# S5 read-out with the chunks as the stationary operand, in two 64-column halves, and transposes behind the GELU

## The chip, the cores and the metric

The kernel runs on one core of one Trainium2 chip. Its time is the device time of one execution, in microseconds (us); the comparison later is between medians of several runs. The engines are named as in the profile: PE is TensorE's matmul side and PEld its weight loads, DVE is VectorE, ACT is ScalarE, POOL is GpSimd, SP is SyncE. POOL and SP issue DMA transfers here. TensorE's clock is granted at one of two levels, 2.4 GHz (1.0 in the profile) or 1.2 GHz (0.5).

## The reference, cut to what matters

Two layers, sequence 512, model width 2048, everything in float32. Each layer normalises and modulates `x`, projects it, runs two branches side by side (S5 state space and differential attention), and projects back. The change lies in the S5 branch:

```python
_, states = lax.associative_scan(combine, (a_seq, bu), axis=1)
c_mat = lax.complex(c_re, c_im)
y = jnp.einsum('gpn,bsgn->bsgp', c_mat, states).real + d_skip * uf
y = jax.nn.gelu(y.reshape(bsz, s, SSM_WIDTH))
ab = y @ w_glu + b_glu
out = ab[..., :SSM_WIDTH] * jax.nn.sigmoid(ab[..., SSM_WIDTH:])
```

There are 64 groups of 16 channels. The kernel cuts the 512 positions into 64 chunks of 8. For one group it needs a 128 x 64 result: 128 rows are 8 positions by 16 channels, 64 columns are the chunks. That result is the sum of two products with a contraction over 128: a table `Mb` (128 x 128, what the inputs of the same chunk give) times the inputs `U` (128 x 64), and a table `O` (128 x 128) times the states `X` at the chunks' starts (128 x 64).

## The kernel before, in words

The order of the work is written by hand. A step (`step`) belongs to one weight unit, a 512 KB tile of weights: SP loads it, ACT rounds it (`hi`), DVE takes the remainder (`lo`), and PE does 24 matmuls with 512 moving columns against it. Units are split three ahead of their use (`NH = 4` buffers). Beside that stream run generators, the S5 branch, the attention and the adaLN modulation. Each advances by one `yield` in each of three phases of a step: ahead of the split, ahead of the matmuls, and behind them. Generators are served by priority, and every engine executes its instructions in the order in which they were recorded.

The read-out is the last part of `s5_state_gen`. It takes the 64 groups in 8 rounds of 8, one round per step; each layer has 8 rounds, so there are 16 in all. In round j:

- In the first phase POOL issues three loads for the next round (`s5_load_be`, `load_m`, `s5_load_u`), and DVE makes the two tables in four operations of 1024 columns: two products and their difference for `O`, and the masking of `Mb`.
- In the second phase `gelu(j - 1)` reads the round before from its PSUM bank (rounds alternate between bank 3 and bank 2): ACT squares and scales, DVE multiplies, ACT takes the tanh, DVE forms the result in `g2`, POOL writes it to DRAM (`yD`).
- In the third phase, behind the 24 matmuls of the step, PE does 16 matmuls of the round: for each of 8 groups `Mb` stationary with `U` moving, then `O` stationary with `X` moving, 64 moving columns each. A float32 matmul shows as two records in the trace, each with its own weight load.

Behind round 7 the generator does one more GELU and sets `o.done`. `ada_chain` waits for `o.done`, then starts `ada_gen` for the gate: a 1 MB broadcast load (`in_bgate`) on POOL, 512 KB loads (`in_wada`) on SP, and DVE sums (`ada_acc`: two operations of 512 columns per tile). The attention of the same layer is running by then. For each head it projects k, q and a gate; `qk_out` copies k or q from PSUM and has SP move its rows by four DMAs (`sb<-sb`), `rope` rotates it on DVE, `qk_split` writes the pieces (`qk`) that the score matmuls read.

Elsewhere in the kernel, at the start of layer 0, `first_cols` uses matmuls with 32 stationary columns that write to the four quarters of a bank's partitions (shown as 128*32 in the trace).

Of the kernel before, what the change touches and what calls it, by code (L numbers as in the profile page):

```python
# [14 lines left out]
AF = mybir.ActivationFunctionType  # L15
# [6 lines left out]
P = 128  # L22
KT = D // P
NG = 64
# [32 lines left out]
SHARED = 8192  # L57
# [10 lines left out]
class Prog:  # L68
# [42 lines left out]
    def v(self, off, n):  # L111
        return self.sb[:, off:off + n]
# [226 lines left out]
def build(ctx, tc, io):  # L339
    q = Prog(ctx, tc, io)  # L340
    nc = q.nc
    M, A, SUB = ALU.mult, ALU.add, ALU.subtract
    v = q.v
    bank = q.bank
# [32 lines left out]
    def layout(base, limit, **sizes):  # L377
        r = Names()
        o = base
        for name, (count, n) in sizes.items():  # L380
            got = []
            for _ in range(count):
                got.append(o)
                o += n
            setattr(r, name, got if count > 1 else got[0])
        assert o <= base + limit, (o - base, limit)
        return r
# [9 lines left out]
    s5 = layout(R5, 4416, U=(2, 512), BE=(2, 384), K=(2, 128), D=(2, 128), PR=(1, 512),  # L397
                PI=(1, 512), GR=(1, 512), GI=(1, 512), A8=(1, 64))
# [3 lines left out]
    s5.A, s5.T = ra.p[0], ra.wt[0] - 128  # L402
    s5.tab = [RA + 2048 + 64 * i for i in range(24)]
    s5.tw = RA + 3584
    sh = layout(0, SHARED, X=(1, NG * 65), A=(1, 1024), B=(2, 1024))

    gl = layout(R5, 4416, gate=(1, D), g=(2, 512), zs=(2, 512))
    yst_o = [RA + 2048 + 512 * i for i in range(8)]
# [219 lines left out]
    def s5_load_be(l, j, lo):  # L628
        q.dma(v(s5.BE[j % 2], 384), io["be"][l, j, :, lo:lo + 384])

    def s5_load_u(l, j):
        src = q.uD[l][j * P:(j + 1) * P, :].rearrange("(g q) (s c) -> (q s) g c", q=16, c=64)
        q.dma(v(s5.U[j % 2], 512).rearrange("p (g c) -> p g c", c=64), src)
# [137 lines left out]
    def s5_state_gen(l):  # L771

        o = S5[l]
        todo = got = 0
        while o.v < 8:
            yield
            if todo > o.v:
                j = o.v
# [11 lines left out]
            j = o.v  # L790
            if j < 8 and o.u > j and o.r > j:
                U = v(s5.U[j % 2], 512)
# [7 lines left out]
        X = o.X  # L800
# [19 lines left out]
        for i, job in enumerate(jobs):  # L820
# [13 lines left out]
            lv, g0, gn, src, dst, n = job  # L834
# [22 lines left out]
        def load_m(j):  # L857
            base = q.kD[l][16384 * j:16384 * (j + 1)]
            src = bass.AP(base.tensor, base.offset, [[16, P], [2048, 8], [1, P]])
            q.dma(o.B[j % 2].rearrange("p (g f) -> p g f", g=8), src)  # L860
# [6 lines left out]
        def gelu(j):  # L867

            b = bank[3 - j % 2]
            g1, g2 = v(s5.g1, 512), v(s5.g2, 512)  # L870
            q.act(g1, b, AF.Square)
            q.act(g1, g1, AF.Copy, scale=0.044715, bias=1.0)
            q.tt(g1, g1, b, M)
            q.act(g1, g1, AF.Tanh, scale=math.sqrt(2.0 / math.pi))
            q.stt(g2, g1, 1.0, b, A, M)
            dst = q.yD[l][8 * j:8 * j + 8].rearrange("g r c -> r g c")
            q.dma(dst, g2.rearrange("p (g c) -> p g c", c=64))

        for j in range(8):
            if j < 7:  # L880
                s5_load_be(l, j + 1, 128)
                load_m(j + 1)
                s5_load_u(l, j + 1)
            be = v(s5.BE[j % 2], 384).rearrange("p (f g q) -> p f g q", f=3, g=8)
            O = o.A[j % 2]
            On4 = O.rearrange("p (g s e) -> p g s e", g=8, s=8)
            T4 = o.T.rearrange("p (g s e) -> p g s e", g=8, s=8)
            pr = PR[:, 8 * j:8 * j + 8, :].unsqueeze(3).to_broadcast([P, 8, 8, 16])
            pi = PI[:, 8 * j:8 * j + 8, :].unsqueeze(3).to_broadcast([P, 8, 8, 16])
            q.tt(On4, pr, be[:, 1].unsqueeze(2).to_broadcast([P, 8, 8, 16]), M)  # L890
            q.tt(T4, pi, be[:, 2].unsqueeze(2).to_broadcast([P, 8, 8, 16]), M)
            q.tt(O, O, o.T, SUB)
            Mb = o.B[j % 2].rearrange("p (g f) -> p g f", g=8)
            q.tt(Mb, Mb, tapb.unsqueeze(1).to_broadcast([P, 8, P]), M)
            yield
            if j > 0:
                gelu(j - 1)
            yield
            b = bank[3 - j % 2]
            U = v(s5.U[j % 2], 512)  # L900
            for g in range(8):
                q.mm(b[:, g * 64:(g + 1) * 64], Mb[:, g], U[:, g * 64:(g + 1) * 64], True, False)
                q.mm(b[:, g * 64:(g + 1) * 64], O[:, g * P:(g + 1) * P], X[:, 8 * j + g, 0:64], False, True)
            yield
        o.read = True
        yield
        gelu(7)
        o.done = True
        yield
        yield  # L910
# [263 lines left out]
    def layer(l):  # L1174
        u0 = l * UL
        last = l == DEPTH - 1
        o = S5[l]
# [45 lines left out]
        def start_s5():  # L1223
            t = q.shared(SHARED, F32, f"ss{l}")
            o.X = t[:, sh.X:sh.X + NG * 65].rearrange("p (g c) -> p g c", c=65)
            o.A = [t[:, sh.A:sh.A + 1024], v(s5.A, 1024)]
            o.T = v(s5.T, 1024)
            o.B = [t[:, b:b + 1024] for b in sh.B]
            o.gen = s5_gen(l)
            o.sgen = s5_state_gen(l)  # L1230
            q.spawn(1, o.gen, True)
            q.spawn(2, o.sgen, True)
# [47 lines left out]
        for j in range(first_u, 8):  # L1280
            b = next_bank()
# [7 lines left out]
        for j in range(8):  # L1289
            b = bank[(1, 0, 7)[j % 3]]  # L1290
# [53 lines left out]
        for h in range(8):  # L1344
# [6 lines left out]
            for kind in range(3):  # L1351
                b = next_bank()
# [351 lines left out]
```

## Time and profile before

| | |
|---|---|
| median of 3 runs | 1929.06 us (1927.9 to 1932.54) |
| profiled execution | 1930.6 us, of it 1928.8 us span |
| PE busy | 1898.0 us, 98% |
| DVE busy | 1352.2 us, 70% |
| ACT busy | 782.8 us, 41% |
| POOL busy | 200.5 us, 10% |
| mean granted TensorE clock | 0.994 |
| read-out rounds, layer 0 | 368.6 to 436.1 us |
| read-out rounds, layer 1 | 1274.0 to 1340.9 us |

Busy time counts an engine as busy as long as any of its instructions is in flight. Matmuls overlap, so the mean duration of one (0.39 us for 512 columns) is longer than the distance from one start to the next (0.23 us). The distance between starts, not the duration, tells what a matmul costs on PE.

### The profile page before, as it was taken

Reading aid. Unit: us, or ns where it says so; the run is one execution under the profiler, and the core shown is the slowest. Engines: PE = TensorE matmul, PEld = TensorE weight load, DVE = VectorE, ACT = ScalarE, POOL = GpSimd, SP = SyncE. Lnnn points to the kernel's source line nnn. Section 1 sums busy time; section 2 is a strip of 40 time slices with the busy share of each in tenths; the row PEclk is TensorE's granted clock in tenths of the full one; section 3 lists DMA queues with packets and bytes.
Section 4 is the critical chain, followed back from the end, with each engine's and each line's share of the span. In section 5 each row is a group of like instructions: output and inputs, shape, how many; then the busy total and the mean of one; then the engine's idle time right before and its main releaser. Section 6 shows DMA issues by size and latency. Waiting matters only on the chain.

```text
span 1928.8 us, 27771 instructions
## 1 busy us (share of the span) xinstructions
PE 1898.0 (98%) x10376; PEld 1613.2 (84%) x10376; DVE 1352.2 (70%) x2590; ACT 782.8 (41%) x1473; POOL 200.5 (10%) x316
## 2 busy tenths in 40 slices
PE   7999999999999999999999999999999999999998
PEld 4678998888888888888998899888788878888887
DVE  7748767987777887688776435796688777653444
ACT  4333234444445554322264224433344445432222
POOL 0003220231000000100001210032000000000000
PEclk8999999999999999999999999999999999999999
DMA  9967553677666964777444433376666584355233
GB/s 353 403 250 250 183 148 95 212 198 219 184 186 187 224 191 166 277 278 231 141 156 148 135 110 108 100 234 203 179 187 199 175 202 133 120 166 200 98 90 119
DMA packets 120695, 358.75 MB, mean 186 GB/s; under 512 B 32272, under 2 KB 32848, under 8 KB 118128
## 3 DMA queue, kind: packets, MB, share of 16 engines
q1 hardware_dynamic: 97776, 277.14, 45.0%
q0 software_dynamic: 22784, 79.84, 13.9%
q8 instruction: 81, 1.33, 0.3%
q14 instruction: 54, 0.44, 0.1%
HBM read 309.60 MB, written 30.54 MB: 176 GB/s over the span
## 4 chain that ended last, share of the span: by engine, by line
PE 87%; DVE 6%; DMA 3%; issue 2%; ACT 1%; SPq 0%; POOL 0%; ACTq 0%; DVEq 0%; POOLq 0%
PE bk L145 86%; DVE lo L130 2%; DVE sb L139 2%; PE bk L153 1%; DVE sb L130 1%; DMA sb<-yD 1%; DMA sb<-sb 1%; DMA sb<-in_ssm_d 0%; DMA sb<-in_wada 0%; DVE sb L134 0%; ACT sd L127 0%; DMA sb<-in_lstep 0%; ACT hi L127 0%; ACT hth L127 0%; DVE x L134 0%
## 5 line engine op out<-in xcount | busy, mean ns | idle before, releaser
L130 DVE TENSOR_TENSOR lo<-sb,hi 128x1024 fp32r<-128x1024 f32 x288 | 351.2, 1222 | 365.8 <-ACT hi L127 349.5
L127 ACT ACTIVATE hi<-sb 128x1024 fp32r<-128x1024 f32 x288 | 304.0, 1059 | 558.8 <-PE bk L145 442.2
L145 PE MATMUL bk<-hth,hi 128*128 128x512 f32 x1280 | 512.7, 401 | 0.0
L145 PE MATMUL bk<-hth,lo 128*128 128x512 f32 x1280 | 500.3, 391 | 0.0
L145 PE MATMUL bk<-htl,hi 128*128 128x512 f32 x1280 | 499.5, 390 | 0.0
L145 PE MATMUL bk<-hi,hth 128*128 128x256 f32 (+1 forms) x1088 | 360.1, 331 | 4.5 <-ACT hth L127 4.1
L145 PE MATMUL bk<-lo,hth 128*128 128x256 f32 (+1 forms) x1088 | 356.0, 327 | 0.5 <-DVE lo L130 0.5
L145 PE MATMUL bk<-hi,htl 128*128 128x256 f32 (+1 forms) x1088 | 356.1, 327 | 0.0
L139 DVE SCALAR_TENSOR_TENSOR sb<-sb 128x512 f32<-128x512 f32 (+8 forms) x633 | 296.1, 473 | 21.4 <-DMA sb<-in_wada 1.8
L145 PEld LDWEIGHTS bk<-hth,lo 128*128 128x128 f32 x1280 | 240.8, 188 | 51.9
L145 PEld LDWEIGHTS bk<-htl,hi 128*128 128x128 f32 x1280 | 241.3, 189 | 49.1 <-issue 1.9
L145 PEld LDWEIGHTS bk<-hth,hi 128*128 128x128 f32 x1280 | 241.3, 189 | 48.2 <-issue 1.9
L130 DVE TENSOR_TENSOR sb<-sb 128x4 f32<-128x4 f32 (+8 forms) x455 | 219.6, 500 | 28.3 <-DMA sb<-sb 10.9
L145 PEld LDWEIGHTS bk<-hi,hth 128*128 128x128 f32 x1088 | 207.1, 190 | 34.4 <-issue 12.0
L145 PEld LDWEIGHTS bk<-hi,htl 128*128 128x128 f32 x1088 | 207.0, 190 | 18.1 <-DVE htl L130 0.5
L145 PEld LDWEIGHTS bk<-lo,hth 128*128 128x128 f32 x1088 | 207.2, 190 | 17.4 <-DVE lo L130 0.7
L145 PE MATMUL bk<-gt,hi 128*128 128x512 f32 x512 | 159.6, 393 | 0.0
L145 PE MATMUL bk<-sb 128*128 128x128 f32 (+5 forms) x932 | 134.0, 338 | 4.3 <-DVE sb L433 3.6
L127 ACT ACTIVATE sb<-bk,sb 128x512 f32<-128x512 f32 (+3 forms) x144 | 77.2, 541 | 132.7 <-DVE sb L134 131.0
L145 PEld LDWEIGHTS bk<-gt,hi 128*128 128x128 f32 x512 | 94.7, 188 | 18.8
L127 ACT ACTIVATE sb<-bk 128x512 f32<-128x512 f32 (+3 forms) x213 | 87.8, 445 | 45.1 <-PE bk L145 35.4
L145 PE MATMUL bk<-gt,lo 128*128 128x512 f32 x256 | 99.8, 390 | 0.0
(116 smaller groups left out, 1744.0 us busy)
## 6 DMA issues: line engine op xcount, KB each, us to landing
sb<-in_w SPq DMA_DIRECT2D x288, 512.0 KB, 4.0
sb<-in_wada SPq DMA_DIRECT2D x185, 512.0 KB, 5.0
sb<-uD POOLq DMA_DIRECT2D x32, 256.0 KB, 6.0
ss<-kD POOLq DMA_DIRECT2D x16, 512.0 KB, 5.9
sb<-sb SPq DMA_DIRECT2D x128, 64.0 KB, 3.9
qk<-qk POOLq DMA_DIRECT2D x32, 256.0 KB, 4.0
sb<-in_be POOLq DMA_DIRECT2D x32, 192.0 KB, 4.3
x<-in_x SPq DMA_DIRECT2D x4, 1024.0 KB, 10.0
```

What stands on the lines that cost most here:

```text
L127: self.nc.scalar.activation(out=out, in_=in_, func=func, **kw)
L130: self.nc.vector.tensor_tensor(out=out, in0=a, in1=b, op=op)
L139: self.nc.vector.scalar_tensor_tensor(out=out, in0=a, scalar=s, in1=b, op0=op0, op1=op1)
L145: return self.nc.tensor.matmul(out, lhsT=l, rhs=r, start=a, stop=z)
L153: return self.nc.tensor.transpose(out, in_, self.ident)
```

## The change

The two operands of each read-out matmul change places: `U` and `X` (128 x 64) become stationary, `Mb` and `O` (128 columns) move. A group's result is now 64 x 128, chunks on the partitions. Of two neighbouring groups the even one is written to partitions 0 to 63 and the odd one to 64 to 127 of the bank, so the two use different 64-column halves of the array. The number of matmuls stays 16 per round.

The GELU is elementwise and works on the bank as it is. Its result then has the wrong layout for `yD`, so four 128 x 128 transposes on PE (`gelu_turn`) write it to the same bank, ACT copies it to a new tile `Y` (`gelu_out`), and POOL sends it from there. `gelu_turn` of a round stands one step later than its GELU, behind the matmuls of the next round. Behind round 7 this takes one more step, and `o.done` is set one step later.

```diff
-    sh = layout(0, SHARED, X=(1, NG * 65), A=(1, 1024), B=(2, 1024))
+    sh = layout(0, SHARED, X=(1, NG * 65), A=(1, 1024), B=(2, 1024), Y=(1, 512))
...
             q.stt(g2, g1, 1.0, b, A, M)
+
+        def gelu_turn(j):
+            for p in range(4):
+                q.tr(bank[3 - j % 2][:, P * p:P * p + P], v(s5.g2 + P * p, P))
+
+        def gelu_out(j):
+            q.act(o.Y, bank[3 - j % 2], AF.Copy)
             dst = q.yD[l][8 * j:8 * j + 8].rearrange("g r c -> r g c")
-            q.dma(dst, g2.rearrange("p (g c) -> p g c", c=64))
+            q.dma(dst, o.Y.rearrange("p (g c) -> p g c", c=64))
...
-            yield
+            if j > 1:
+                gelu_turn(j - 2)
+            yield
+            if j > 1:
+                gelu_out(j - 2)
             if j > 0:
                 gelu(j - 1)
             yield
...
-            for g in range(8):
-                q.mm(b[:, g * 64:(g + 1) * 64], Mb[:, g], U[:, g * 64:(g + 1) * 64], True, False)
-                q.mm(b[:, g * 64:(g + 1) * 64], O[:, g * P:(g + 1) * P], X[:, 8 * j + g, 0:64], False, True)
+            for p in range(4):
+                for i in range(2):
+                    for g in (2 * p, 2 * p + 1):
+                        r = b[64 * (g % 2):64 * (g % 2) + 64, P * p:P * p + P]
+                        if i == 0:
+                            q.mm(r, U[:, g * 64:(g + 1) * 64], Mb[:, g], True, False)
+                        else:
+                            q.mm(r, X[:, 8 * j + g, 0:64], O[:, g * P:(g + 1) * P], False, True)
             yield
         o.read = True
-        yield
+        gelu_turn(6)
+        yield
+        gelu_out(6)
         gelu(7)
+        yield
+        yield
+        gelu_turn(7)
+        yield
+        gelu_out(7)
         o.done = True
```

PE, layer 0, before: the end of round 1 (bank 2, `bk_78`) and the start of the next step's matmuls (`hth`, `htl`: the layer's input; `hi`, `lo`: the weight unit; `ss`, `sb`: tables, states and inputs).

```order
L145 MATMUL bk_78<-sb,ss_1106 128x64
L145 MATMUL bk_78<-ss_1106,sb 128x64
L145 MATMUL bk_77<-hth,hi_68 128x512
L145 MATMUL bk_77<-htl,hi_68 128x512
L145 MATMUL bk_77<-hth,lo_72 128x512
```

PE, the same place now.

```order
L145 MATMUL bk_78<-ss_1106,sb 64x128 x2
L145 MATMUL bk_78<-sb,ss_1106 64x128 x2
L153 MATMUL bk_79<-sb 128x128 x4
L145 MATMUL bk_77<-hth,hi_68 128x512
L145 MATMUL bk_77<-htl,hi_68 128x512
L145 MATMUL bk_77<-hth,lo_72 128x512
```

A row with x2 is a pair of neighbouring groups in the two halves. The four transposes (L153) of round 0, in bank 3, have come in between round 1 and the next step's stream.

DVE, layer 1, before: the first head's q behind the read-out. `sb<-sb x3` is `rope`, `lo` the split of a weight unit, `sb<-sb` of L134 and L139 the sums of `ada_acc`, `qk` is `qk_split`.

```order
L130 TENSOR_TENSOR sb<-sb 128x512 x3
L130 TENSOR_TENSOR lo_71<-sb,hi_67 128x1024
L134 TENSOR_SCALAR sb<-sb 128x512
L139 SCALAR_TENSOR_TENSOR sb<-sb 128x512 x3
L130 TENSOR_TENSOR qk_10083<-sb,qk_10083 64x512 x2
L130 TENSOR_TENSOR lo_72<-sb,hi_68 128x1024
```

DVE, the same place now.

```order
L130 TENSOR_TENSOR sb<-sb 128x512 x3
L130 TENSOR_TENSOR lo_71<-sb,hi_67 128x1024
L130 TENSOR_TENSOR qk_10137<-sb,qk_10137 64x512 x2
L130 TENSOR_TENSOR lo_72<-sb,hi_68 128x1024
L139 SCALAR_TENSOR_TENSOR sb<-sb,bk_77 128x512
L134 TENSOR_SCALAR sb<-sb 128x512
L139 SCALAR_TENSOR_TENSOR sb<-sb 128x512 x3
```

The four sums of `ada_acc` stood ahead of `qk_split`; now they stand behind it, one weight unit later.

SP, layer 1, before: the same stretch (L1358 the four row moves of `qk_out`, `in_w` weight units, `in_wada` the tiles of `ada_gen`).

```order
L1358 DMA sb<-sb 32x512 x4
L315 DMA sb<-in_w 128x1024
L531 DMA sb<-in_wada 128x1024 x2
L315 DMA sb<-in_w 128x1024
L1358 DMA sb<-sb 32x512 x4
L315 DMA sb<-in_w 128x1024
L531 DMA sb<-in_wada 128x1024 x2
```

SP, the same place now (L1383 is the line of the row moves there).

```order
L1383 DMA sb<-sb 32x512 x4
L315 DMA sb<-in_w 128x1024 x2
L1383 DMA sb<-sb 32x512 x4
L531 DMA sb<-in_wada 128x1024 x2
L315 DMA sb<-in_w 128x1024 x2
L531 DMA sb<-in_wada 128x1024 x2
```

The first two tiles of `ada_gen` were issued ahead of the second group of row moves and are now issued behind it.

## Rows read from the trace of the kernel before

**Rows 1.** The page: its head, busy times, the chain by engine.

```profile
span 1928.8 us, 27771 instructions
...
PE 1898.0 (98%) x10376; PEld 1613.2 (84%) x10376; DVE 1352.2 (70%) x2590; ACT 782.8 (41%) x1473; POOL 200.5 (10%) x316
...
PE 87%; DVE 6%; DMA 3%; issue 2%; ACT 1%; SPq 0%; POOL 0%; ACTq 0%; DVEq 0%; POOLq 0%
```

**Rows 2.** Timeline, PE, one read-out round of layer 1: start us, us, what.

```profile
1300.93 0.39 PE L145 MATMUL bk<-hth,lo 128*128 128x512 f32 x1
1301.15 0.33 PE L145 MATMUL bk<-sb,ss 128*128 128x64 f32 x2
...
1304.45 0.39 PE L145 MATMUL bk<-ss,sb 128*128 128x64 f32 x2
1304.64 0.48 PE L145 MATMUL bk<-hth,hi 128*128 128x512 f32 x1
1304.96 0.39 PE L145 MATMUL bk<-htl,hi 128*128 128x512 f32 x1
```

**Rows 3.** Timeline, PE, matmuls of first_cols in four 32-column quarters.

```profile
69.22 0.40 PE L145 MATMUL bk<-hi,htl 128*128 128x512 f32 x1
69.55 1.92 PE L145 MATMUL bk<-sb 128*32 128x512 f32 x16
...
71.73 0.39 PE L145 MATMUL bk<-lo,hth 128*128 128x512 f32 x1
```

**Rows 4.** Timeline, weight loads, of the same stretch.

```profile
69.54 0.16 PEld L145 LDWEIGHTS bk<-sb 128*32 128x32 f32 x8 [0.36 <-issue]
70.00 0.13 PEld L145 LDWEIGHTS bk<-sb 128*32 128x32 f32 x4 [0.30 <-issue]
70.43 0.13 PEld L145 LDWEIGHTS bk<-sb 128*32 128x32 f32 x4 [0.30 <-issue]
```

**Rows 5.** Timeline, PE, attention: float32 matmuls of 128 columns, then transposes (L153).

```profile
1441.39 0.39 PE L145 MATMUL bk<-hth,lo 128*128 128x512 f32 x1
1441.62 0.83 PE L145 MATMUL bk<-sb 128*128 128x128 f32 x6
1442.28 0.60 PE L153 MATMUL bk<-sb 128*128 128x128 f32 x4
...
1442.95 0.40 PE L145 MATMUL bk<-htl,hi 128*128 128x512 f32 x1
```

**Rows 6.** Timeline, DVE, a step of the read-out: in brackets idle time and its releaser.

```profile
1294.71 1.22 DVE L130 TENSOR_TENSOR lo<-sb,hi 128x1024 fp32r<-128x1024 f32 x1
...
1297.10 0.69 DVE L130 TENSOR_TENSOR sb<-sb,bk 128x512 f32<-128x512 f32 x1 [0.58 <-ACT sb L127]
1298.49 0.69 DVE L139 SCALAR_TENSOR_TENSOR sb<-sb,bk 128x512 f32<-128x512 f32 x1 [0.70 <-ACT sb L127]
1299.10 1.22 DVE L130 TENSOR_TENSOR ss<-sb 128x1024 f32<-128x1024 f32 x1
```

**Rows 7.** Timeline, ACT, the same step: a copy from PSUM, the GELU's square.

```profile
1293.03 0.58 ACT L127 ACTIVATE sb<-bk 128x512 f32<-128x512 f32 x1
1295.81 0.60 ACT L127 ACTIVATE sb<-bk 128x512 f32<-128x512 f32 x1 [2.20 <-PE bk L145]
```

**Rows 8.** Timeline, DVE, layer 1, behind the read-out.

```profile
1359.16 2.02 DVE L130 TENSOR_TENSOR sb<-sb 128x512 f32<-128x512 f32 x3 [9.12 <-DMA sb<-sb]
...
1362.23 0.48 DVE L134 TENSOR_SCALAR sb<-sb 128x512 f32<-128x512 f32 x1
1362.75 2.33 DVE L139 SCALAR_TENSOR_TENSOR sb<-sb 128x512 f32<-128x512 f32 x3
1365.11 1.40 DVE L130 TENSOR_TENSOR qk<-sb,qk 64x512 fp32r<-64x512 f32 x2
```

**Rows 9.** Timeline, PE, the same stretch.

```profile
1362.53 0.39 PE L145 MATMUL bk<-hth,lo 128*128 128x512 f32 x1
1365.85 1.41 PE L145 MATMUL bk<-qk 128*128 128x128 f32 x4 [2.93 <-DVE qk L130]
```

**Rows 10.** Timeline, SP: the row moves of the second projection.

```profile
1349.18 4.45 SPq L1358 DMA_DIRECT2D sb<-sb  x4
```

**Rows 11.** Timeline, POOL: the broadcast of the gate's bias.

```profile
1345.63 0.56 POOL L142 DMA_DIRECT2D sb<-in_bgate  x1
```

**Rows 12.** Busy time by stretch (PE, PEld, DVE, ACT, POOL), granted clock, DMA share, GB/s.

```profile
1366.00:1372.00 6.00, 5.97 (x17) 4.81 (x18) 5.50 (x9) 1.28 (x4) 0.00 (x0) 0.50 0.84 254
```

More of the change, by code (lines that the diff above doesn't have):

```diff
@@ L1227, in start_s5 @@
             o.T = v(s5.T, 1024)
+            o.Y = t[:, sh.Y:sh.Y + 512]
             o.B = [t[:, b:b + 1024] for b in sh.B]
```

## The prediction

> **What bounds the kernel now.** I read the page first: PE is busy 98% of the span and carries 87% of the chain that ended last; DVE, the next, is busy 70% [rows 1]. So what the change does to PE's time counts in full as long as nothing else becomes late. Then the timeline of PE inside a read-out round, for what a round costs; then the places of the trace that resemble the new round: matmuls in quarters of the array, and transposes. Then DVE and ACT in the same step, to see whether they can follow a faster PE. Last the one place behind the read-out where PE really stood idle, because the change moves instructions there.
>
> A round now stands between a stream matmul that starts at 1300.93 and the second one behind the round at 1304.96, 4.03 us apart [rows 2]. Without the round two stream steps of about 0.225 us would lie there (1300.93 to 1301.15 is 0.22), so the round costs 4.03 - 0.45 = 3.58 us, or 0.112 us for each of its 32 records. Sixteen rounds are 57.3 us. The reader should notice that this price is not set by the moving columns: records with 128 moving columns come just as fast. Six of them and four transposes, inserted in the same way, cost 1442.95 - 1441.39 - 0.45 = 1.11 us, 0.111 us each [rows 5]. What both have in common is the load of 128 stationary columns. A matmul that moves only 64 columns against 128 stationary ones therefore wastes the array, and exchanging the operands halves the loads.
>
> **The new round.** It again has 16 matmuls, 32 records, with 64 stationary and 128 moving columns. No row has 64-column halves. The nearest are the quarters at the start of the kernel: 16 records of 512 columns, four quarters at a time, cost 71.73 - 69.22 - 0.45 = 2.06 us [rows 3]. Their loads come in bundles of four at 70.00 and 70.43 [rows 4], so a bundle of four records takes 0.43 us, four bundles 1.72 us, and 0.34 us is left for changing into the quartered array and back. Two things follow. Different column tiles run at once, at least when there are four. And the eight loads stamped from 69.54 within 0.16 us lie under the first bundle of matmuls, so the next loads are hidden.
>
> Carried over to halves: 16 records deep, each at the 0.111 us of a 128-column record [rows 5], is 1.78 us; with 0.34 us for the change of tiling, 2.12 us. That is 3.58 - 2.12 = 1.46 us less a round, 23.4 us over 16. Bounds: if the change of tiling costs nothing in this place, 1.78 us and 5.4 us more gain; if the halves take turns, 32 x 0.111 + 0.34 = 3.89 us, dearer than now. I take 2.12, since rows 3 show both the overlap and the cost of changing.
>
> The transposes are new on PE: 4 a round, 64 in all, at 0.11 us [rows 5] 7.0 us. They stand in PE's own order, so nothing hides them. PE's net is 23.4 - 7.0 = 16.4 us less.
>
> **Can the others follow?** A step with a read-out becomes 5.4 (24 stream matmuls) + 2.12 + 0.44 = 8.0 us; it is 9.0 now. DVE has per step four table operations and one split at no more than 1.22 us, 6.1 us, and the GELU from 1297.10 to 1299.10, 2.0 us with its wait for the tanh [rows 6]; every second step also has the z gate, about 0.7 us. That is 8.1 or 8.8 us at most: a deficit of up to 0.45 us a step on average, some 3 us over the six steps between a layer's first and last round. The lead is larger: the split at 1294.71 stands behind all table operations, and the round that needs those tables starts at 1301.15 [rows 2, 6], 6.4 us later. So DVE's lateness doesn't reach PE within 8 rounds. I count nothing; without the lead it would cost up to 6 us over both layers.
>
> The transposes add a wait: PE must have the GELU's result. Behind a waiting transpose stands the whole weight stream, so a late GELU costs in full. The square starts at 1295.81 and the result is ready at 1298.49 + 0.69 = 1299.18, 3.4 us later [rows 6, 7]. In the new order ACT first copies out the round before: four transposes of 0.44 us, a copy of 0.58 us [rows 7], 0.2 us to get going, so the result is ready 0.44 + 0.58 + 0.2 + 3.4 = 4.6 us behind the round's end. PE comes to its transposes 8.0 us behind it, and behind the last round, where no round intervenes, 5.9 us. Slack 3.4 and 1.3 us: no wait. The new copies are 16 x 0.58 us on an engine that waits 2.2 us for PE in such a step [rows 7]. The `yD` send moves the same bytes, a little earlier in POOL's queue than the late wait it has now. Each costs nothing.
>
> **What moves behind the read-out.** `o.done` is a step later, and with it all of `ada_gen`. In layer 1 this meets PE's only long stall behind the first layer's start. The row moves of the second projection are issued slowly, 4.45 us for four [rows 10], just behind the 1 MB broadcast [rows 11]; DVE waits 9.12 us for them, then does `rope`, a split, four `ada_acc` sums (1362.23 to 1365.08) and only then `qk_split` at 1365.11 [rows 8]. PE, free at about 1362.9, waits 2.93 us for it [rows 9]. Its clock, at the 2.4 GHz level until then, is granted at 0.50, the 1.2 GHz level, in the 6 us behind [rows 12], which loses 3 us. The stall costs about 6 us.
>
> In the changed order the four sums stand behind `qk_split`. If the row moves land as late as today relative to PE, `qk_split` starts at 1362.23 instead of 1365.11 on the old scale, 2.88 us earlier, and PE's wait shrinks from 2.93 us to nearly nothing, without the fall of the clock. The landing may shift: the first two 512 KB tiles are now issued behind these row moves, which helps, but the broadcast comes later too and then runs beside them, which hurts. I take the wait as all but gone, with 0.5 us left, and a gain of 5.5 us; ends: 0 (the row moves land 3 us later, or a stall of that size opens elsewhere in the attention) and 6.
>
> **Sum.** The profiled execution took 1930.6 us, 1928.8 of it span, and lies 1.5 us above the median of 1929.06. 1930.6 - 16.4 - 5.5 = 1908.7; on the scale of the medians 1907.
>
> **Rivals.**
>
> A. The stall stays, or its like opens in the attention of either layer, whose `ada_acc` sums all move by a step. For it: DMA traffic around the row moves is as dense as before. Against it: the order itself puts 2.85 us of DVE work behind the waiting `qk_split`. Time: 1929 - 16.4 = 1912.7, with a second stall up to 1919.
>
> B. The loads of a half are not hidden. From rows: the 0.112 us of a record with 64 moving columns bound a load of 128 columns, so 64 columns take up to 0.056 us; exposed in each half, 16 x (0.111 + 0.056) + 0.34 = 3.01 us a round. That saves 9.1 us and the transposes take 7.0: 1927 without the stall's gain, some 1924 with part of it. Against it: in the quarters the second loads lie under running matmuls [rows 4], and full-width records of 128 columns keep 0.111 us although load and stream each need most of it [rows 5]. The Trainium skill ("TensorE: Matmul & The Clock Gate", "The mechanism") speaks for B: it says that a weight load overlaps a running matmul only when the two use different row groups, and both halves here use all rows. By that rule the change would be worth almost nothing; rows 4 contradict it for quarters.
>
> C. The other side: the halves take turns. The mechanism is one queue of records in which the second record of a group's matmul holds up the neighbour's first. Then 32 x 0.111 + 0.34 = 3.89 us a round, 0.31 us dearer, 5.0 us in all, and the transposes add 7.0: 1929 + 12 = 1941, or 1935.5 if the stall goes as well. It decides when fewer than 7 of a round's 16 pairs overlap (above 3.14 us a round, what it saves no longer pays the transposes' 0.44). Against it: rows 3 cost 4 records' time for 16, and there too each matmul has two records. For it: those were long records of 512 columns, issued in bundles of four; here 32 short ones must be issued in 1.78 us, 0.056 us apart, and no row shows a steady pace below 0.109 us.
>
> **How the numbers follow.** Forecast 0.55, own range 1902 to 1911 (the change of tiling cheaper, the stall fully gone; or 0.2 us more a round). A 0.27, up to 1919. B 0.08. C 0.08. Some other wait that cancels the gain 0.02. From 1902 to 1919 nearly all of the forecast and A are held, 8 in 10. A difference under 0.3%, 5.8 us, can't be told from no change here. Faster by more than that: forecast, A and a little of B, 0.84. Within: most of B and the odd wait, 0.08. Slower: C, 0.08.
>
> **What the changed profile would show.** A round with its change of tiling costs 2.1 us between the same two stream matmuls, and its 32 records start in pairs a few ns apart; about 3 us means B, 3.9 means C. Four transposes behind each round from the third on, 0.44 us, with no idle time of PE ahead of them; idle time there released by DVE means that I misjudged the GELU's slack. Steps of 8.0 us in both layers. No fall of the granted clock behind layer 1's read-out, and the first `qk` score matmuls without a wait above 1 us; otherwise A. The forecast is wrong at its root if the rounds take less time but the span doesn't follow.

## The result and the profile after

The changed kernel takes 1919.26 us (median of 4 runs, 1918.29 to 1919.86), the kernel before 1930.61 us (4 runs): ratio 0.9942, 95% interval 0.9930 to 0.9954. It is 11 us faster, half of the 22 us that were forecast. The head of the page after, its busy times and its chain by engine answer to [rows 1]:

```profile
span 1917.8 us, 27929 instructions
...
PE 1883.1 (98%) x10440; PEld 1590.0 (83%) x10440; DVE 1350.5 (70%) x2590; ACT 788.0 (41%) x1489; POOL 200.8 (10%) x316
...
PE 74%; DVE 13%; DMA 6%; issue 4%; ACT 3%; POOL 0%; SPq 0%; ACTq 0%; DVEq 0%; POOLq 0%
```

PE is as busy as before, but the chain that ended last now runs for 13% of the span through DVE (6% before) and for 6% through DMA (3%). So in some places something other than PE decides. The round itself is not one of them: its matmuls stand back to back. The timeline of PE, a round of layer 1, answers to [rows 2]; a form `128*64` is a matmul with 64 stationary columns, and x4 counts records:

```profile
1303.66 0.39 PE L145 MATMUL bk<-hth,lo 128*128 128x512 f32 x1
1303.98 0.44 PE L145 MATMUL bk<-ss,sb 128*64 128x128 f32 x4
1304.25 0.39 PE L145 MATMUL bk<-ss 128*64 128x128 f32 x4
...
1305.56 0.39 PE L145 MATMUL bk<-ss 128*64 128x128 f32 x4
1305.88 0.66 PE L153 MATMUL bk<-sb 128*128 128x128 f32 x4
1306.29 0.48 PE L145 MATMUL bk<-hth,hi 128*128 128x512 f32 x1
1306.61 0.39 PE L145 MATMUL bk<-htl,hi 128*128 128x512 f32 x1
```

Four records take 1304.25 - 1303.98 = 0.27 us at first and 0.22 us from then on, where four records of the old round took 0.45 us. From 1303.66 to the second stream matmul behind it, less 0.45 us as in [rows 2], round and transposes cost 2.50 us. The first round of a layer has no transposes and costs 2.10 us, so four transposes cost about 0.40 us. Sixteen rounds give back 16 x (3.58 - 2.10) = 23.7 us, and 16 x 0.40 = 6.4 us go to transposes: 17.3 us less on PE. The weight loads of the same stretch, which answer to [rows 4]:

```profile
1303.98 0.20 PEld L145 LDWEIGHTS bk<-ss,sb 128*64 128x64 f32 x4 [0.35 <-issue]
1304.14 0.25 PEld L145 LDWEIGHTS bk<-ss 128*64 128x64 f32 x4
1304.36 0.25 PEld L145 LDWEIGHTS bk<-ss,sb 128*64 128x64 f32 x4
```

The loads for the next four records start at 1304.14, while the matmuls stamped from 1303.98 still run. The pace says the same: with B's loads in the open a round would have cost 3.01 us, not 2.10. The sentence of the Trainium skill that spoke for B ("TensorE: Matmul & The Clock Gate", "The mechanism": a load overlaps running matmuls only when the row groups differ) doesn't hold in this trace, since all these tiles use all 128 rows.

Now where 6 of the 17.3 us went. In layer 0 two groups of transposes wait for the GELU, and behind the second the stream is slow. Timeline of PE, layer 0, changed kernel; the bracket is idle time and its releaser:

```profile
411.53 0.66 PE L153 MATMUL bk<-sb 128*128 128x128 f32 x4 [1.12 <-DVE sb L139]
...
422.68 0.66 PE L153 MATMUL bk<-sb 128*128 128x128 f32 x4 [3.10 <-DVE sb L139]
...
424.31 0.63 PE L145 MATMUL bk<-htl,hi 128*128 128x512 f32 x1
424.74 0.63 PE L145 MATMUL bk<-hth,lo 128*128 128x512 f32 x1
```

Stream matmuls start 0.43 us apart there instead of 0.227. The granted clock is 0.50 (the 1.2 GHz level) for 3.4 us from 423.8 on, after PE's idle time, and 1.00 (2.4 GHz) up to it. At half the clock, half of 3.4 us is lost, so the two waits and the clock cost 1.12 + 3.10 + 1.7 = 5.9 us. What DVE did before the second wait, from its timeline:

```profile
411.39 1.22 DVE L130 TENSOR_TENSOR ss<-sb 128x1024 f32<-128x1024 f32 x1
412.53 1.22 DVE L130 TENSOR_TENSOR sb<-sb 128x1024 f32<-128x1024 f32 x1
413.78 2.36 DVE L130 TENSOR_TENSOR ss<-ss,sb 128x1024 f32<-128x1024 f32 x2
416.06 1.40 DVE L130 TENSOR_TENSOR qk<-sb,qk 64x512 fp32r<-64x512 f32 x2
417.49 2.02 DVE L130 TENSOR_TENSOR sb<-sb 128x512 f32<-128x512 f32 x3
419.42 1.22 DVE L130 TENSOR_TENSOR lo<-sb,hi 128x1024 fp32r<-128x1024 f32 x1
420.56 0.68 DVE L130 TENSOR_TENSOR sb<-sb,bk 128x512 f32<-128x512 f32 x1
421.93 0.69 DVE L139 SCALAR_TENSOR_TENSOR sb<-sb,bk 128x512 f32<-128x512 f32 x1 [0.69 <-ACT sb L127]
```

Here DVE stands still only for the 0.69 us of the Tanh. Between the tables and the GELU it does `qk_split` (1.40 us) and `rope` (2.02 us) of the first head: a step of 11.1 us, on an engine that feeds a PE step of 8.0. In layer 0 the read-out runs beside the first head's projections; the rows I read for DVE [rows 6] were of layer 1, in a step that has neither.

In layer 1 the stall of [rows 8, 9] is still there. Timeline of all engines, changed kernel, behind the read-out of layer 1 (rows of SP and POOL are issues of DMAs):

```profile
1338.48 3.15 SPq L1383 DMA_DIRECT2D sb<-sb  x4
...
1338.98 0.56 POOL L142 DMA_DIRECT2D sb<-in_bgate  x1
...
1351.68 2.02 DVE L130 TENSOR_TENSOR sb<-sb 128x512 f32<-128x512 f32 x3 [12.00 <-DMA sb<-sb]
...
1354.86 1.41 DVE L130 TENSOR_TENSOR qk<-sb,qk 64x512 fp32r<-64x512 f32 x2
...
1355.60 1.41 PE L145 MATMUL bk<-qk 128*128 128x128 f32 x4 [2.92 <-DVE qk L130]
...
1358.55 2.33 DVE L139 SCALAR_TENSOR_TENSOR sb<-sb 128x512 f32<-128x512 f32 x3
```

The `ada_acc` sums did go behind `qk_split`, as the order said (now at 1358.55). But the row moves landed 10.1 us after the last of them was issued (1341.63 to 1351.68), where it was 5.5 us before (1353.63 to 1359.16 [rows 8, 10]). The broadcast now goes out beside them (1338.98; it stood 3.5 us ahead of them, at 1345.63 [rows 11]). PE waits 2.92 us again, and the clock behind it is again 0.50 for 6.8 us, which loses 3.4 us.

A measure for both layers is the time from the first round's first row to the first row of the first head's scores, read from the timeline of PE in each run. Layer 0: 368.6 to 432.0 before, 368.9 to 430.2 after, 63.4 and 61.3 us. Layer 1: 91.9 and 83.1 us. So layer 1 gave 8.8 us and layer 0 only 2.1. The experiments below use this measure ("stretch 0" and "stretch 1"). It ends at the first scores, so what is lost or given back behind them needs a longer one. From the same timelines, of one profiled execution each (us; e4 to e15 are the experiments below):

| | first round of layer 0 starts at | from there to the first round of layer 1 | from there to the second head's first scores in layer 1 |
|---|---|---|---|
| before | 368.62 | 905.35 | 134.36 |
| e6 (before, broadcast later) | 370.77 | 905.34 | 129.20 |
| e15 (e6 and mask on ACT) | 370.98 | 905.72 | 129.42 |
| changed | 368.93 | 903.61 | 125.71 |
| e4 (changed, rope of one head left out) | 367.91 | 899.71 | 123.54 |
| e5 (changed, broadcast later) | 369.40 | 903.63 | 119.80 |
| e13 (e5 and mask on ACT) | 369.54 | 897.64 | 120.71 |

Where an edit touches nothing, the stretches agree within a few hundredths (905.35 and 905.34, 903.61 and 903.63). The start of the first round differs by up to 3 us, ahead of what these edits change in the read-out; why stays open, and the time of a whole run contains it.

### The profile page after: what moved, and what is told of

The parts are those of the page before. It is cut to its first block, busy times and chain, and to the rows that moved or that the text cites. A ratio compares the mean times of both kernels' runs of the same rounds, so it can differ in the third digit from the quotient of the medians.

```text
span 1917.8 us, 27929 instructions
## 1 busy us (share of the span) xinstructions
PE 1883.1 (98%) x10440; PEld 1590.0 (83%) x10440; DVE 1350.5 (70%) x2590; ACT 788.0 (41%) x1489; POOL 200.8 (10%) x316
## 4 chain that ended last, share of the span: by engine, by line
PE 74%; DVE 13%; DMA 6%; issue 4%; ACT 3%; POOL 0%; SPq 0%; ACTq 0%; DVEq 0%; POOLq 0%
PE bk L145 72%; DVE sb L130 4%; DVE lo L130 3%; DVE sb L139 3%; PE bk L153 2%; DMA sb<-in_wada 1%; DMA sb<-in_w 1%; DVE ss L130 1%; ACT hi L127 1%; DMA x<-in_x 1%; DMA sb<-in_ssm_d 1%; ACT sb L127 1%; DMA sb<-sb 1%; DVE sb L134 1%; DMA vD<-sd 0%
## 5 line engine op out<-in xcount | busy, mean ns | idle before, releaser
L139 DVE SCALAR_TENSOR_TENSOR sb<-sb 128x512 f32<-128x512 f32 (+7 forms) x633 | 295.5, 473 | 21.4 <-DMA sb<-in_wada 2.0
L145 PEld LDWEIGHTS bk<-hth,hi 128*128 128x128 f32 x1280 | 241.6, 189 | 48.7 <-issue 2.3
L145 PE MATMUL bk<-sb 128*128 128x128 f32 (+6 forms) x932 | 134.1, 340 | 4.8 <-DVE sb L433 3.9
L127 ACT ACTIVATE sb<-sb 128x128 f32<-128x128 f32 (+2 forms) x163 | 62.7, 413 | 89.7 <-DVE sb L130 54.7
```

Source lines behind the costliest of these rows:

```text
L127: self.nc.scalar.activation(out=out, in_=in_, func=func, **kw)
L139: self.nc.vector.scalar_tensor_tensor(out=out, in0=a, scalar=s, in1=b, op0=op0, op1=op1)
L145: return self.nc.tensor.matmul(out, lhsT=l, rhs=r, start=a, stop=z)
```

## Experiments

The edits are shown shortened. `mask` stands for the broadcast 0/1 table that `Mb` is multiplied with, `tapc` for its values per partition, one column for each block of 16 columns.

**What holds layer 0.** *e4*: rope of the first head of layer 0 left out.

```
-def rope(kind):
+def rope(kind, skip=False):       # skip: layer 0, head 0
...
+    if skip: return
```

> The changed kernel without the three rope instructions of each of q and k of the first head of layer 0 (4.0 us of DVE; the rotation is left out there); all else is as it was. Theory DVE: the backlog of 4.2 us that the two waits of layer 0 show falls by 4.0 us, the waits and the clock's fall go but for a few tenths; 1913 to 1914.5. Rival ACT (GELU late by its own chain or by ACT): the two waits stay, 1919 to 1920.

Measured 1912.26 us, ratio 0.9909 (0.9892 to 0.9925). Stretch 0 is 55.8 us, 5.5 less; its one wait for the GELU is 0.46 us, another of 1.37 us comes behind the scores, and the clock doesn't fall there. Up to the first round of layer 1 that makes 3.9 us less (899.71 against 903.61), for 4.0 us of DVE work left out. DVE's load, not ACT. (The whole is 0.7 us below theory DVE's range; layer 1's stall was 1.99 us here with nothing changed there.)

*e1* and *e9*: without the transposes.

```
-    q.tr(bank[3 - j % 2][:, P * p:P * p + P], v(s5.g2 + P * p, P))
-    q.act(o.Y, bank[3 - j % 2], AF.Copy)        # e1: Y gone, yD stored from g2
+    q.act(o.Y, v(s5.g2, 512), AF.Copy)          # e9: copy kept
```

> The changed kernel without its 64 transposes and 16 copies of them; GELU's result is stored in the order in which the round leaves it. It has two waits of 1.12 and 3.10 us ahead of transposes in layer 0 (410.4 and 419.6 us) and a stretch of 3.4 us at a granted clock of 0.50 behind them, 5.9 us in all. Theory DVE (the engine has more work in these steps than a step is long, whatever waits for it): the transposes' own 0.39 us a round go (-6.2 us), but the read-out matmuls of the last two rounds now wait for their masks instead, by my sum 2.4 and 3.7 us; 1911 to 1914. Rival LATENCY (only the transposes ask for GELU's result so early, nothing else is late): no wait of more than 0.4 us in the read-out of layer 0, 1907 to 1908. The stall of 2.9 us behind layer 1's read-out stays in both.

Measured 1927.79 us, ratio 0.9990 (0.9980 to 0.9999): 8.5 us slower than the changed kernel, which neither theory had. Timeline of e1, layer 1:

```profile
1306.97 0.69 DVE L139 SCALAR_TENSOR_TENSOR sb<-sb,bk 128x512 f32<-128x512 f32 x1 [5.07 <-DMA yD<-sb]
...
1312.38 0.44 PE L145 MATMUL bk<-ss,sb 128*64 128x128 f32 x4 [4.25 <-DVE ss L130]
```

GELU's tile can't be written again until its store has landed, and with a step of 7.5 us that is too late; DVE waits, and PE with it. In layer 0 the rounds waited 1.35 and 2.09 us for their masks, a little over half of my sums of 2.4 and 3.7, but with e1's own wait beside it that settled nothing; e9 keeps the copy.

> The changed kernel without its 64 transposes, but with ACT's copy into the staging tile kept (from GELU's result), so that the stores don't hold GELU's tile. In the run without the copy DVE waited up to 5.7 us for a store of y to land (three times in layer 1), which hid what was asked. Theory DVE (the first scores of layer 0 start when DVE has done its work, whatever PE does): from the first round to the first scores of layer 0 about 60 us as with transposes (61.3 us), in layer 1 3.1 us less; 1915.5 to 1917.5. Rival LATENCY (only the transposes ask for GELU's result early): layer 0 gains its 5.9 us of waits and clock and 3.1 us of transposes; 1907 to 1909.

Measured 1916.18 us, ratio 0.9917 (0.9899 to 0.9934). Stretch 0 is 60.0 us: taking 6 x 0.40 = 2.4 us from PE in it gave 1.3. PE waits 1.48 us for a mask and then, in its timeline,

```profile
430.19 0.69 PE L145 MATMUL bk<-qk 128*128 128x128 f32 x2 [5.42 <-DVE qk L130]
```

Up to the first round of layer 1 it takes 904.2 us, no less than the changed kernel's 903.6. So the lateness is not the transposes'. Without them the same backlog is met at a mask and at q. Stretch 1 is 80.5 us, 2.6 less. LATENCY falls.

*e2*: GELU first. The GELU's DVE instructions stand around the mask, ahead of rope, split and weight correction.

```
+    if j > 1: gelu_turn(j - 2); gelu_out(j - 2)
+    if j > 0: gelu_a(j - 1)          # square .. tanh
     q.tt(Mb, Mb, mask, M)
+    if j > 0: gelu_b(j - 1)          # last product
-    if j > 1: gelu_turn(j - 2)
     yield
-    if j > 1: gelu_out(j - 2)
-    if j > 0: gelu(j - 1)
```

> The changed kernel with GELU of round j-1 put ahead of rope, split and weight correction in DVE's order (in the first third of a step in place of the second), its two DVE instructions around the mask of M, so that ACT's Tanh runs under the mask. Theory DVE: the 0.7 us of DVE idle a step goes and rope and split no longer stand ahead of GELU; the two waits of layer 0 (4.2 us) and the clock's fall (1.7 us) go, a wait of about 1.2 us for the mask of the last round is left; 1914 to 1916. Rival ACT (GELU is late by its own chain of four ACT and two DVE instructions, or by ACT's order): waits as before, 1919 to 1920. The stall of layer 1 stays in both.

Measured 1920.30 us, ratio 0.9952 (0.9937 to 0.9967), above theory DVE's 1914 to 1916. Both waits went, and PE waited 4.75 us for q instead. Stretch 0 is 60.1 us. I took this for the backlog met at another place; that is only half true. The copy of the transposes now stands on ACT ahead of the copy of q, and waits for PE:

```profile
404.78 0.60 ACT L127 ACTIVATE ss<-bk 128x512 f32<-128x512 f32 x1 [3.87 <-PE bk L153]
...
408.77 0.58 ACT L127 ACTIVATE sb<-bk 128x512 f32<-128x512 f32 x1
```

The copy of q at 408.77 comes 38.0 us behind the first round; in the changed kernel it was 33.0 (401.90), so the row moves and the split are later by my own edit.

*e7*: GELU first, broadcast behind the scores (e5 below), mask on GpSimd.

```
-    q.tt(Mb, Mb, mask, M)
+    nc.gpsimd.tensor_tensor(out=Mb, in0=Mb, in1=mask, op=M)
```

> The changed kernel with GELU first as in that run, the mask of M (128x1024, 1.22 us a step on DVE) done by GpSimd, and the broadcast behind the scores. With GELU first alone the waits inside the read-out of layer 0 went, but a wait of 4.75 us for the first head's qk took their place. Theory DVE (layer 0 is bound by the sum of DVE's work from the read-out to the first scores): 7 x 1.22 = 8.5 us less on DVE clear the backlog of 4 to 5 us; no wait above 0.5 us in layer 0, no fall of the clock there; with the broadcast moved 1907 to 1910. Rival PORT (GpSimd takes over 3 us for a mask or makes DVE's instructions longer than 1.22 us): the rounds wait for the mask, 1913 to 1920.

Measured 1922.39 us, ratio 0.9957 (0.9940 to 0.9973); PE waits 2.17 us for a mask and 7.24 us for q. Timeline of DVE and POOL:

```profile
409.63 2.18 POOL L912 TENSOR_TENSOR ss<-ss,sb 128x1024 f32<-128x1024 f32 x1
...
410.58 0.69 DVE L139 SCALAR_TENSOR_TENSOR sb<-sb,bk 128x512 f32<-128x512 f32 x1 [0.70 <-ACT sb L127]
...
417.14 3.72 DVE L130 TENSOR_TENSOR ss<-ss,sb 128x1024 f32<-128x1024 f32 x1
417.59 2.18 POOL L912 TENSOR_TENSOR ss<-ss,sb 128x1024 f32<-128x1024 f32 x1
```

The mask takes 2.2 us on GpSimd, and a DVE instruction beside it 3.72 us in place of 1.22, as if it had stood still for the mask; one with an operand in PSUM (410.58) keeps its 0.69. PORT held, at a time 2.4 us above its range. Not all of the wait for q is the port's: with GELU first, as in e2, the copy of q comes 40.4 us behind the first round here (411.40). The Trainium skill ("SBUF — State Buffer", "Who interferes with whom") says this of DVE instructions with two SBUF inputs, and the trace agrees, with 2.5 us more for the DVE instruction.

*e13*: broadcast behind the scores, mask on ACT. Here DVE loses 1.22 us a step and no order changes. *e15* makes both edits in the kernel before.

```
-    q.tt(Mb, Mb, mask, M)
+    for s in range(7):
+        q.act(Mb[:, :, 16*s:16*s+16], Mb[:, :, 16*s:16*s+16], AF.Copy, scale=tapc[:, s:s+1])
```

> The changed kernel with the broadcast behind the scores and the mask of M made by seven ACT instructions of 128x128 with a scale per partition in place of one on DVE (1.22 us a step less on DVE; by the rows of 128x128 copies about 2.5 us a step more on ACT, which is busy 3.3 to 4.2 us of 8). Theory DVE: by the time of the first head's q DVE has some 6 us less to do in layer 0; the waits for GELU (1.1 and 3.3 us) fall to under 1 us in all and the clock does not fall; 1908 to 1911 against 1915.3 with the broadcast alone. Rival CHAIN (the lateness is of row moves, ACT's order or GELU's own chain, and ACT now has more): layer 0 still takes 60 us or more from the first round to the first scores; 1914 to 1919.

> The kernel before with the broadcast behind the scores and the mask on ACT. Theory DVE: there a step is 9.0 us, DVE kept up and PE waited for nothing in layer 0, so it gives nothing over the broadcast alone (1928.0 us): 1927 to 1929. Rival ANYWAY (less DVE work is worth the same 5 us in either kernel): 1922 to 1924.

Measured: e13 1908.99 us (1907.94 to 1909.23), ratio 0.9886 (0.9869 to 0.9902), the fastest of all; e15 1927.11 us, ratio 0.9978 (0.9969 to 0.9987), which is e6's 1928.0 within the measurement. So DVE's load is worth 6.3 us below e5 in the changed kernel (6.0 of it from the first round of layer 0 to that of layer 1) and nothing that can be told in the kernel before: stretch 0 is 63.4 us in e15 as it was, though DVE works 51.0 us in it in place of 56.9. The busy times by stretch show it; the rows are a kernel's last part of stretch 0 (from the seventh round to the scores) and the sum over all of it (us, then busy PE, PEld, DVE, ACT, POOL, granted clock, DMA share, GB/s). Before:

```profile
423.00:432.00 9.00, 9.00 (x57) 8.07 (x56) 8.80 (x10) 3.96 (x7) 0.95 (x1) 1.00 0.63 130
sum 63.40, PE 63.40 PEld 56.55 DVE 56.90 ACT 24.05 POOL 20.45; mean PE 9.06 PEld 8.08 DVE 8.13 ACT 3.44 POOL 2.92
```

The changed kernel:

```profile
417.60:430.20 12.60, 9.50 (x61) 7.86 (x61) 11.74 (x14) 4.93 (x8) 3.14 (x4) 0.86 0.57 146
sum 61.30, PE 57.05 PEld 46.74 DVE 56.65 ACT 26.31 POOL 21.20; mean PE 8.15 PEld 6.68 DVE 8.09 ACT 3.76 POOL 3.03
```

e13:

```profile
416.90:424.80 7.90, 7.90 (x62) 6.76 (x62) 7.07 (x9) 6.98 (x15) 1.51 (x2) 1.00 0.50 136
sum 55.30, PE 55.30 PEld 45.65 DVE 48.65 ACT 40.73 POOL 21.08; mean PE 7.90 PEld 6.52 DVE 6.95 ACT 5.82 POOL 3.01
```

DVE has 56.7 us of work in stretch 0, and with six waits of 0.70 us for a Tanh 60.9 us. Before, PE needed 63.4 us, so DVE just fitted. The changed round asks 55.3 us of PE, and the stretch takes the 61.3 us in which DVE does its work almost without a gap. With the mask elsewhere DVE has 48.7 us of work, PE never waits, and the stretch is the 55.3 us of seven steps of 7.9. The price of DVE's lateness is thus 6.0 us.

The slow clock is a part of this price and not an extra one. In the changed kernel the split of q ends at 428.71, and PE, slow until 427.2, comes to the scores at 430.24. In e5, which is the same up to there, PE waits 1.14 and 3.28 us for the same two GELUs, the clock stays at 1.00, and PE then waits for a third one, behind the scores:

```profile
433.15 0.66 PE L153 MATMUL bk<-sb 128*128 128x128 f32 x4 [1.37 <-DVE sb L139]
```

That is 5.8 us where the changed kernel lost 5.9, and both reach layer 1 after 903.6 us. Why the clock fell behind a wait of 3.10 us in the one and not behind 3.28 us in the other is open.

*e14*: e13 with GELU first and one of O's instructions between its two.

> As that run, with GELU first in DVE's order and one of O's instructions between its two (nothing of DVE waits for Tanh). Theory DVE: 2 us a step less than in the changed kernel, no wait above 0.5 us in layer 0's read-out; 1907 to 1910, no more than 2 us below the run with the mask on ACT alone. Rival CHAIN: a wait for q of 3 us or more ahead of the first scores of layer 0, since split stands behind the last O in DVE's order and the row moves land late; 1912 to 1917.

Measured 1918.52 us, ratio 0.9937 (0.9921 to 0.9953). PE waits 4.49 us for q, as CHAIN had it, at a time 1.5 us above CHAIN's range. The copy of q is at 411.26 us, 40.5 behind the first round, against 33.4 in e13. GELU first is a bad order, with the mask on ACT or not. The traces point to what it puts in front of q on ACT; that was not tested by itself.

**What holds layer 1.** *e3*, *e5*, *e6*: the broadcast of the gate's bias later.

```
-    if gate: q.dma(v(gl.gate, D), bgate)                 # POOL, ahead of the first load
+    if gate and i == 2: q.dma(v(gl.gate, D), bgate)      # e3: POOL, two steps later
+    if gate and k == 2: nc.sync.dma_start(..., bgate)    # e5, e6: SP, behind the third load
```

> The changed kernel with the 1-MB broadcast of the gate's bias issued two steps later in both layers; nothing else moves. In layer 1 the four row moves issued at 1338.5 to 1341.7 us land only at 1351.6 us. Theory COLLISION (the broadcast, issued at 1339.0, holds them up): they land within 4 to 7 us, the stall of 2.92 us behind layer 1's read-out and the 6.8 us at a granted clock of 0.50 behind it go; -5 to -6.5 us, 1913 to 1914.5. Rival WEIGHTS (the two loads of ada weights and the other transfers on the queues hold them up, not the broadcast): they land after 9 us or more, the stall keeps 2 us or more, 1918 to 1920. The waits in layer 0 stay in both.

Measured 1916.40 us, ratio 0.9931 (0.9916 to 0.9946). POOL has nothing to wait for there, so the issue moved only from 1339.0 to 1342.3; the row moves landed 6.5 us after the last was issued, the stall fell to 1.18 us. The time lies between the two theories' ranges.

> The changed kernel with the broadcast of the gate's bias issued by SP behind the third load of ada weights instead of by POOL ahead of the first; in the run with the late broadcast POOL ran ahead and had issued it at 1342.3 us, 3.4 us later than before and still among the row moves, so that run did not part the theories. Theory COLLISION (the broadcast holds up the row moves of the first head's k and q): the moves issued at about 1339 to 1342 us land within 7 us, no wait of PE for qk above 0.5 us behind layer 1's read-out and no fall of the clock there; 1913 to 1914.5. Rival WEIGHTS (the other transfers of that burst suffice: two loads of ada weights, w, qk's halves, v, the last y): landing after 9 us or more, a stall of 1 us or more; 1915.5 to 1918. Layer 0's waits of 4.2 us stay in both.

> The same edit on the kernel before: the broadcast issued by SP behind the third load of ada weights. Its stall behind layer 1's read-out is 2.93 us with 6.8 us at a granted clock of 0.50 behind it. COLLISION: the stall is under 0.5 us, no fall of the clock; -5 to -6 us, 1924 to 1926. WEIGHTS: stall of 1 us or more; 1927 to 1931. What the edit gives here and in the changed kernel should be about the same, so that the change's own gain stays at 11 us; if it gives much more in one, the change has moved the stall's cause.

Measured: e5 1915.27 us, ratio 0.9922 (0.9907 to 0.9936); e6, on the kernel before, 1928.00 us, ratio 0.9986 (0.9976 to 0.9995). In e5 nothing waits, from its timeline:

```profile
1338.97 3.41 SPq L1383 DMA_DIRECT2D sb<-sb  x4
...
1347.95 2.02 DVE L130 TENSOR_TENSOR sb<-sb 128x512 f32<-128x512 f32 x3 [7.78 <-DMA sb<-sb]
...
1353.01 0.56 PE L145 MATMUL bk<-qk 128*128 128x128 f32 x4
```

Landing 5.6 us after the last issue instead of 10.1, no wait, no fall of the clock, stretch 1 80.0 us. COLLISION holds for the changed kernel by these rows. (The edit moves the broadcast in time and to another queue at once; e3, which kept the queue, points the same way.) In the kernel before the stall falls from 2.93 to 0.44 us. The whole gains only 4.0 us in e5 and 2.5 in e6, less than COLLISION had, but the stage itself gains what a stall with its slow clock was said to cost: to the second head's scores 125.71 becomes 119.80 us in e5 (5.9 less) and 134.36 becomes 129.20 in e6 (5.2 less). Most of what is missing in e6's whole is the later start of its first round in the profiled execution, 370.77 against 368.62, where the edit changes nothing.

**Other tests.** *e8*: both groups of a pair in columns 0 to 63.

```
-    r = b[64 * (g % 2):64 * (g % 2) + 64, P * p:P * p + P]
+    r = b[0:64, P * p:P * p + P]
```

> The changed kernel with both groups of a pair in columns 0 to 63 of the array (both write the lower half of the bank, one sum over the two, so the result is not the reference's); number, size and order of matmuls unchanged. Theory HALVES (the two halves of the array work at the same time; that is where the round's 2.10 us come from): records take turns at 0.109 us each, a round goes to 32 x 0.109 + 0.35 = 3.8 us, 16 rounds cost 28 us more in rounds, some of it hidden by the waits of layer 0; 1940 to 1948. Rival LOADS (the pace is that of the 64-column weight loads or of the records themselves, wherever they go): 2.1 us a round, 1918 to 1921.

Measured 1941.44 us, ratio 1.0060 (1.0045 to 1.0075). Timeline of PE, a round:

```profile
1321.60 0.60 PE L145 MATMUL bk<-ss 128*64 128x128 f32 x4
1322.04 0.60 PE L145 MATMUL bk<-ss,sb 128*64 128x128 f32 x4
```

Four records take 0.44 us instead of 0.22; steps are 9.7 us instead of 7.96, which makes the round 3.85 us, near the 3.89 of rival C. HALVES holds: the gain is the two halves at work together.

*e10*, *e11*, *e12*: every head's attention a step later, in the changed kernel, with GELU first, and in the kernel before.

```
-    q.spawn(0, attn_gen(l, h))
+    q.later(1, lambda: q.spawn(0, attn_gen(l, h)))
```

> The changed kernel with every head's attention started one step (5.45 us) later; nothing else moves. Theory DVE and COLLISION: both stalls ahead of a first head's scores are lateness of its q, so the stall of layer 1 (2.92 us, and the clock's fall behind it) goes; in layer 0 the two waits of the transposes for GELU (4.2 us and 1.7 us of clock) stay, since they stand ahead of the scores; 1913 to 1915.5. Rival ORDER (the scores only uncover the next wait, or the later attention ends later and holds up the gated unit behind it): 1917 to 1921.

> GELU first in DVE's order, and every head's attention one step later. Theory DVE: GELU first took away the waits inside the read-out of layer 0 and left one of 4.75 us for the first head's q, which the later attention covers; layer 1's stall goes too. No wait above 0.5 us from the first round to the first scores in either layer; 1907 to 1910, what the prediction had for the change. Rival BOUND (DVE's work delays whatever comes next on PE, the last round's mask or the weights): 1913 to 1918.

> The kernel before with every head's attention one step later. Its stall of layer 1 (2.93 us and 6.8 us of half clock) goes, layer 0 had no wait; 1924 to 1926.5. With the run of both edits on the changed kernel this gives the change's price on ground without stalls: by the round and transposes as measured 16 x 1.48 - 64 x 0.098 = 17.4 us. If it is 11 us again, the rounds' saving itself is smaller than the trace says.

Measured 1927.39 us (ratio 0.9987, 0.9976 to 0.9999), 1925.89 us (0.9983, 0.9971 to 0.9995) and 1935.69 us (1.0021, 1.0012 to 1.0031). The edit costs 5 us by itself in the kernel before. New waits come late in the attention, in e12 for example:

```profile
677.17 0.38 PE L145 MATMUL bk<-sb 128*128 128x128 f32 x1 [1.70 <-ACT sb L127]
...
746.70 0.50 PE L145 MATMUL bk<-qk 128*128 128x512 f32 x1 [2.13 <-ACT sb L127]
```

All three times lie above every range on record for them. ORDER named what happened, and the runs say little about the change: e12 less e10 is 8.3 us, with different stalls in each. In e11 the last round of layer 0 waits 3.55 us. BOUND had foretold such a wait; the trace names a copy on ACT as its end, and DVE's mask ends 0.1 us ahead of it, so these rows don't part the two.

## Why the prediction was wrong

**The round and the transposes: right.** 2.10 us against 2.12, 0.40 against 0.44 us for four transposes; PE's net gain 17.3 us against 16.4. B and C are excluded by the round, and e8 shows C's price.

**"No wait" and "I count nothing" for DVE: wrong, 5.9 us.** This is the first failed step. Two things in it. I worked out the GELU's slack (3.4 us) along ACT's chain in a step in which DVE had stood idle ahead of the GELU. Where DVE doesn't idle, the GELU is ready when its turn comes in DVE's queue. In layer 1, DVE's last product for the round of 1296.02, from its timeline:

```profile
1304.23 0.69 DVE L139 SCALAR_TENSOR_TENSOR sb<-sb,bk 128x512 f32<-128x512 f32 x1 [0.70 <-ACT sb L127]
```

The result is there at 1304.92, 7.1 us behind the end of its round and not 4.6, and the transposes, which wait for nothing, start at 1305.88: a slack of 1.0 us in place of 3.4. And I took DVE's deficit of 0.45 us a step and its lead of 6.4 us from layer 1 and used them for "both layers". In layer 0 `rope`, split and `rope` fall into two of the steps, 5.4 us in all, more than the slack there. e4 and e13 show that it is this load; e15 shows that the kernel before had no such price. The words "without the lead it would cost up to 6 us over both layers" had the size by luck: the sum behind them spreads the loss over both layers, and all of it fell in layer 0, by work that the sum did not contain.

**The stall behind layer 1's read-out "all but gone": wrong, 5.5 us.** The second failed step. What the order shows came true, the sums went behind the split. The end of the range that I set aside, row moves landing 3 us later, came true too: 4.5 us more between issue and landing, because the broadcast now runs beside them (e3, e5). I had written that it "hurts" and gave it no price. The stall's own price, about 6 us, was right: where its cause is taken away (e5), the stage takes 5.9 us less.

So half of A happened: its stall stayed. Its second stall, in the attention by the moved `ada_acc` sums, did not come; the second loss was the wait for the GELU, which the prediction had excluded. That the time came out at A's end, 1919, is luck. The terms now add up: -17.3 + 5.9 + 0 = -11.4 us against -11.0 by the spans and -11.35 by the medians. With both obstacles out of the way in both kernels the medians give the change 1927.11 - 1908.99 = 18.1 us (e15, e13). By the two columns of the table it is 8.1 + 8.7 = 16.8 us, near the 17.3 of PE's rows; e15 has a wait of 2.52 us later in layer 1 (1583.36) that e13 doesn't have, and that counts in the medians. Open is why the stall of layer 1 was 1.99 us in e4 and 3.52 us in e2, where nothing near it had been changed; the landing of the row moves varies from program to program.

## What to carry to other kernels

When a step of the bottleneck engine is shortened, add up the other engines' work over the whole stretch from the first shortened step to the next point where the results meet, in each stage of the program separately; a lead read in one stage says nothing of another that carries extra work. A slack has to be worked out along the queue of the engine that produces the result, not along the chain of its inputs. And where a change moves a large transfer, look at what small, urgent transfers are issued beside it at the new time, and give that a price.

## What the hardware showed that was not expected

- Two halves of 64 stationary columns, each fed by its own matmul over all 128 rows, run at once: a round of 32 records takes 2.10 us, and 3.85 us when both use the same half.
- A GpSimd product of 128x1024 takes 2.2 us, and a DVE product beside it 3.72 us instead of 1.22.
- Four row moves of 64 KB each land 5.6 us after issue, or 10.1 us with a 1 MB broadcast issued beside them.
- Seven ACT instructions of 8 x 16 elements a partition, each with its own scale, take 2.15 us, where one of DVE over the whole tile takes 1.22: dearer by itself, and 6 us cheaper in the kernel.
